# The second FFN product by sevens: results started by ScalarE, the residual added in the third to sixth products

## The chip, the core and the metric

The kernel is one program on one core of a Trainium2 chip. A core has five engines that run their own queues in order and meet through semaphores: TensorE (PE in the profile; its weight loads are shown as PEld), VectorE (DVE), ScalarE (ACT), GpSimd (POOL) and SyncE (SP, which here issues nearly all DMAs). The metric is the device time of one execution in microseconds (us); lower is better.

## What is computed

The reference is one layer of a hybrid decoder on 1024 prompt tokens and 64 sample tokens, all in float32, with D_MODEL = 1024 and D_FF = 2816:

```python
def swiglu(x, w_in, w_out):
    gu = x @ w_in
    g, u = gu[..., :D_FF], gu[..., D_FF:]
    return (jax.nn.silu(g) * u) @ w_out

x = x + 0.5 * swiglu(rmsnorm(x, norm_ffn1[l]), ffn1_w_in[l], ffn1_w_out[l])
mix, ... = token_mixing(rmsnorm(x, norm_mix[l]), ...)   # pooling branch and Mamba-2 SSD branch, gated
x = x + mix
x = x + 0.5 * swiglu(rmsnorm(x, norm_ffn2[l]), ffn2_w_in[l], ffn2_w_out[l])
y = rmsnorm(x, norm_final)
```

The change touches the last step of both FFNs: the product `(silu(g) * u) @ w_out`, its factor 0.5, and the residual `x + ...`.

## The kernel before

**Layout.** Activations stand transposed, features on the 128 partitions, tokens along the row. The 1088 tokens are held in two halves: h = 0 has 512 tokens, h = 1 has 576 (512 prompt tokens and the 64 sample tokens). A result of an FFN is therefore 8 row blocks m = 0..7 in two halves, 16 tiles `C[m, h]`.

**Precision.** Each float32 operand is split into a rounded high part and the remainder, and a product is three matmuls: high by high, low by high, high by low. The split of a tile costs one ACT instruction (the high part) and one DVE or POOL subtraction (the low part).

**Second product by sevens.** `second` (line 765) computes the product with 7 block products in place of 8 (a Strassen scheme over two halves of the features, of the outputs and of the tokens). The order is `ORDER2 = "4251736"`; in this document a product is called by its digit, so the first is "4" and the fifth is "7". Every product is done in two passes, m0 = 0 and m0 = 2. A pass runs over 11 contraction tiles kk in six steps of two (the last of one); per kk it has 12 matmuls of 272 columns, 132 in a pass, into four PSUM banks. Per FFN there are 14 passes, and the kernel has two FFNs.

What a pass needs and who brings it:

- Weights (`second_weights`, lines 745 to 763): for each step one or two 256 KB blocks are loaded by SP (line 751, tile `wraw`, 6 buffers); two blocks are added or subtracted on POOL (line 757, tile `ws`, 4 buffers; "3" and "4" need one block and no sum); ACT makes the high part `wh` (line 761) and DVE the low part `wl` (line 762), 3 buffers each.
- Operands (`fetch_x`, lines 770 to 791): for each kk one 272 KB tile is loaded by SP (line 784, tile `hr`, or `hp` for the products in `IN_PAIRS`, which have 8 tiles of their own for it), then split by ACT (line 774) and DVE, for "6" POOL (line 775). A product's 11 operands are loaded and split while the product before it runs. `hr` and its high part `hh` come from a pool of 42 tiles (`act`); one product without pairs takes 22 of them.
- Results (`add`, lines 800 to 807): after a pass, DVE adds each PSUM bank, times plus or minus 0.5, into one or two of the 16 tiles `C` (`scalar_tensor_tensor`, 10 or 12 instructions after a pass of most products, 120 for an FFN). `INTO2` says where a product goes. Since DVE only ever adds, `C` must hold the residual before the first result comes.
- Residual (`residual`, lines 793 to 798): it allocates the 16 tiles `C` (from the stage's pool `fx` of 17) and loads the saved x into them from `xspill` in DRAM, 8 loads of 256 KB and 8 of 288 KB, during "4"; both passes of "4" end with all their residual loads issued.

**Who sets the order.** The kernel keeps a small clock `pe[0]` of its own that counts 272/2400 us for a 272-column matmul (14.96 us for a pass) and interleaves generators by due times on it (`start`, `tick`): `X_AT` and `X_PACE` say when the next product's loads begin and how far apart they are, `X_LAG` how many loads a tile's split stays behind its own load. The tile framework then fixes each engine's queue when the program is built: an instruction goes into its queue when the framework expects its inputs and its buffers to be ready, and the earlier one in the code goes first where several are. On the chip each queue is then strictly in order: an instruction that waits holds all behind it.

**After the product.** When "7" is done, half 0 of the result is final and `after(0, ...)` is called; in FFN 1 that is `after1` (line 960), which starts the next RMSNorm of half 0 beside the last two products (`norm_parts`, line 937, with `rstd`, line 382: squares on ACT, their sums on DVE, a matmul with ones, a reciprocal root on POOL, and then for each of 8 tiles a scaling and a split). `HN_AT` and `HN_PACE` set its due times. When "3" is done, FFN 2 calls `half`.

Of the kernel before, what the change touches and what calls it, by code (L numbers as in the profile page):

```python
# [11 lines left out]
AF = mybir.ActivationFunctionType  # L12
ALU = mybir.AluOpType

P = 128
D = 1024
# [13 lines left out]
HALVES = (0, 1)  # L30
NTOK = (512, 576)
# [14 lines left out]
STEP_S = 1.0  # L46
POST, RIPE = 1.0, 3.0
GP = (1.5, 1.2)
HN_AT, HN_PACE = 3.0, 3.2
MP = 2.0  # L50
R_WAIT0 = 3.5
R_WAIT = 0.5
# [8 lines left out]
ORDER2 = "4251736"  # L61
# [3 lines left out]
INTO2 = {"1": ((0, 0, 1), (1, 1, 1)), "2": ((1, 0, 1), (1, 1, -1)), "3": ((0, 1, 1), (1, 1, 1)),  # L65
         "4": ((0, 0, 1), (1, 0, 1)), "5": ((0, 0, -1), (0, 1, 1)), "6": ((1, 1, 1),), "7": ((0, 0, 1),)}
IN_PAIRS = "457"
LO_POOL = "6"
X_AT, X_PACE, X_LAG = 4.0, 2.0, 2
SUM_PACE = 1.5  # L70


# [1 line left out]
def tile_hybrid_pool_ssd_macaron(  # L74
# [10 lines left out]
    V, S, T, G = nc.vector, nc.scalar, nc.tensor, nc.gpsimd  # L85
    dma = nc.sync.dma_start
# [7 lines left out]
    def nm(s):  # L94
        uid[0] += 1
        return f"{s}_{uid[0]}"

    def act(shape=(P, 576), dt=F32, name="a"):
        return sp.tile(list(shape), dt, tag="act", bufs=N_ACT, name=nm(name))

    def pair(n, name="hl"):
        t = sp.tile([P, 2, 576], F32R, tag="pair", bufs=N_PAIR, name=nm(name))
        return t[:, 0, :n], t[:, 1, :n], t
# [16 lines left out]
    def fx(dt=F32, name="x"):  # L120
        if stage["name"] == "mix":
            return act((P, 576), dt, name)
        return stage["p"].tile([P, 592], dt, tag="fx", bufs=N_FX, name=nm(name))
# [22 lines left out]
    def start(gen, delay=0.0):  # L146
        c = Chain(gen, delay)
        chains.append(c)
        return c
# [13 lines left out]
    def finish(c):  # L163
        while not c.done:
            c.step()
# [33 lines left out]
    def row_vec(src1d, n):  # L199
        rows.append((src1d, n))  # L200
        return sum(r[1] for r in rows[:-1])
# [3 lines left out]
    i_gm = row_vec(norm_mix[0], KD)  # L205
# [56 lines left out]
    xspill = [[dp.tile([P, NTOK[h]], F32, tag=f"xs{h}_{m}", name=f"xspill{h}_{m}") for m in range(KD)] for h in HALVES]  # L262
# [10 lines left out]
    xnd = [dp.tile([P, NTOK[0]], F32, tag=f"xn{k}", name=f"xnd{k}") for k in range(KD)]  # L273
# [490 lines left out]

    def second(wo, after, half):

        X, C = {p: [] for p in ORDER2}, {}
        n = 2 * NQ

        def fetch_x(p, kks, pace, lag=X_LAG):  # L770
            loaded = []

            def part_x(t, a):
                S.activation(a[:, :n], t[:, :n], AF.Identity)
                (G if p in LO_POOL else V).tensor_tensor(t[:, :n].bitcast(F32R), t[:, :n], a[:, :n].bitcast(F32), op=ALU.subtract)
                X[p].append((a, t.bitcast(F32R)))

            for kk in kks:
                if p in IN_PAIRS and kk < N_PAIR:
                    a, t, _ = pair(576, "hp")  # L780
                    t = t.bitcast(F32)
                else:
                    t, a = act((P, 576), F32, "hr"), act((P, 576), F32R, "hh")
                dma(t[:, :n], xq[p][kk])
                loaded.append((t, a))
                if len(loaded) > lag:
                    part_x(*loaded.pop(0))
                yield pace
            while loaded:
                part_x(*loaded.pop(0))  # L790
                yield pace

        def residual(ms):
            for m in ms:
                for h in HALVES:
                    C[m, h] = fx(name="x")
                    dma(C[m, h][:, : NTOK[h]], xspill[h][m])
                yield 1.0

        def add(pt, m, side, c, sign):  # L800
            if side:
                to = [(1, NA + NQ * c, 0, NQ)]
            else:
                to = [(0, 0, 0, NQ)] if c == 0 else [(0, NQ, 0, NQ - NA), (1, 0, NQ - NA, NA)]
            for h, at, of, w in to:
                o = C[m, h][:, at : at + w]
                V.scalar_tensor_tensor(o, pt[:, of : of + w], 0.5 * sign, o, op0=ALU.mult, op1=ALU.add)  # L807

        finish(start(fetch_x(ORDER2[0], range(NKK - 1), 0.0)))
        ahead = []  # L810
        for at, p in enumerate(ORDER2):
            if at + 1 < len(ORDER2):
                last = at + 2 == len(ORDER2)
                ahead.append(start(fetch_x(ORDER2[at + 1], range(NKK), 1.4 if last else X_PACE), 15.0 if last else X_AT if at else 6.0))
            for m0 in (0, 2):
                pts = [[psum("ps" if j and m0 and at < 5 else "pd", "po") for _ in range(2)] for j in range(2)]
                for kp in range(0, NKK, 2):
                    n2 = min(2, NKK - kp)
                    W2 = second_weights(wo, p, kp, n2, m0)
                    for j in range(2):  # L820
                        for k in range(n2):
                            while len(X[p]) <= kp + k:
                                ahead[at - 1].step()
                            xh, xl = X[p][kp + k]
                            for i, (w, x) in enumerate(((0, xh), (0, xl), (1, xh))):
                                for c in range(2):
                                    mm(pts[j][c][:, :NQ], W2[w][:, k, j * P : (j + 1) * P], x[:, c * NQ : (c + 1) * NQ],
                                       start=kp + k == 0 and i == 0, stop=kp + k == NKK - 1 and i == 2)
                            tick()
                    if at == 0 and kp == 2:  # L830
                        while summing:
                            finish(summing.pop())
                        if m0 == 0:
                            finish(start(fetch_x(p, range(NKK - 1, NKK), 0.0)))
                        res = start(residual((0, 4, 1, 5) if m0 == 0 else (2, 6, 3, 7)))
                if at == 0:
                    finish(res)
                with tc.high_priority(HP_EV):
                    for j in range(2):
                        for c in range(2):  # L840
                            for y, side, sign in INTO2[p]:
                                add(pts[j][c], 4 * y + m0 + j, side, c, sign)
            if p == "7":
                after(0, [C[m, 0] for m in range(KD)])
            if p == "3" and half:
                half(1, [C[m, 1] for m in range(KD)])
        after(1, [C[m, 1] for m in range(KD)])
# [86 lines left out]
            for k in range(4):  # L934
                dma(xspill[h][q * 4 + k], x[k][:, : NTOK[h]])

    def norm_parts(xt, h, gi, out, pace=1.0, away=None):

        N = NTOK[h]
        rr = []  # L940
        yield from rstd([t[:, :N] for t in xt], h, D, rr, pace)
        hi, lo, xn, hl = [], [], [], []
        for k in range(KD):
            x = fx(name="xn") if k >= 4 and not away else act((P, 576), name="xn")
            a, b, both = (act((P, 576), F32R, "hi"), act((P, 576), F32R, "lo"), None) if h else pair(576)
            V.scalar_tensor_tensor(x[:, :N], xt[k][:, :N], cols[:, gi + k : gi + k + 1], rr[0], op0=ALU.mult, op1=ALU.mult)
            split(x[:, :N], a[:, :N], b[:, :N])
            hi.append(a)
            lo.append(b)
            xn.append(x)  # L950
            hl.append(both)
            yield pace
            if away:
                dma(away[k], x[:, :N])
        out.append((h, hi, lo, xn, hl))

    wi1 = ffn1_w_in[0]
    prep1m = [None, None]

    def after1(h, xt):  # L960
        o = []
        if h == 0:
            prep1m[0] = start(norm_parts(xt, 0, i_gm, o, HN_PACE, xnd), HN_AT), o

        def away():
            for m in range(KD):
                dma(xspill[h][m], xt[m][:, : NTOK[h]])
                yield 2.0

        start(away(), 5.0)  # L970
        if h == 1:
            finish(prep1m[0][0])
            _, hi, lo, _, hl = prep1m[0][1][0]
            xn = [fx(name="xn") if k >= 4 else act((P, 576), name="xn") for k in range(KD)]
            for k in (0, 4, 1, 5, 2, 6, 3, 7):
                dma(xn[k][:, : NTOK[0]], xnd[k])
            prep1m[0][1][0] = (0, hi, lo, xn, hl)
            prep1m[1] = start(norm_parts(xt, 1, i_gm, o, 1.2), 0.5), o
# [814 lines left out]
    for h in HALVES:  # L1793
# [4 lines left out]
        if h == 1:  # L1798
            o = []
            prep2.append((start(norm_parts(reload(0), 0, i_g2, o, 2.0)), o))  # L1800
            c = prep2[0][0]
# [135 lines left out]
```

## Time and profile before

| | us |
|---|---|
| median of three runs | 2913.13 |
| the three runs | 2914.48, 2904.26, 2913.13 |
| the profiled execution, its own time | 2910.03 |
| span of its profile, first to last instruction | 2908.2 |
| PE busy in the span | 2790.9 (96%) |
| DVE / ACT / POOL busy | 1867.1 / 1396.1 / 1396.3 |

The span is what the profile's engines are measured in; the profiled execution took 1.8 us more than its span. The second product of FFN 1 runs from 528.20 to 794.32 us of the span, that of FFN 2 from 2627.48 to 2892.47. In the rows of the profile L12 means line 12 of the kernel printed above, `out<-in` names the tiles written and read, and an idle time is put down to the instruction or DMA that ended it.

### The profile page before, as it was taken

How to read it: one execution, taken by the hardware profiler on the slowest of the kernel's cores; microseconds unless marked ns; L12 is line 12 of the kernel's file. 1: busy time of each engine (PE TensorE's matmuls, PEld its weight loads, DVE VectorE, ACT ScalarE, POOL GpSimd, SP SyncE). 2: the span in 40 equal slices, each digit the busy share in tenths (PEclk: the TensorE clock that was granted, in tenths of full speed). 3: DMA queues.
4: the chain of work that ended last, by engine and by line, in shares of the span. 5: the costliest groups of instructions: out<-in, count | busy, mean ns of one | idle time of the engine just before them, and what ended most of it. 6: DMA issues, size and time to landing. Idle time of an engine off the chain costs nothing. (4 is left out here: it accounts for less than half of the span.)

```text
span 2908.2 us, 54642 instructions
## 1 busy us (share of the span) xinstructions
PE 2790.9 (96%) x19834; PEld 2613.8 (90%) x19834; DVE 1867.1 (64%) x2938; ACT 1396.1 (48%) x3070; POOL 1396.3 (48%) x1428
## 2 busy tenths in 40 slices
PE   7999999899999999999999999899999999998997
PEld 5999999898889999999988887678999999998997
DVE  6555555685784486876766776875665454557744
ACT  5444444443354555554556566566233434444433
POOL 6566667353642365554622332332135666673424
PEclk9999999999999999999999999899999999999999
DMA  4565554896745455554376677786765332338845
GB/s 138 178 206 195 171 167 142 275 290 209 226 122 167 141 174 169 173 160 135 102 239 215 197 233 234 253 259 185 249 234 166 102 105 90 97 120 299 281 147 173
DMA packets 515791, 539.49 MB, mean 186 GB/s; under 512 B 41780, under 2 KB 356008, under 8 KB 515512
## 3 DMA queue, kind: packets, MB, share of 16 engines
q1 hardware_dynamic: 515504, 535.99, 57.3%
q8 instruction: 156, 2.56, 0.4%
q14 instruction: 115, 0.94, 0.1%
q10 hardware_dynamic: 16, 0.00, 0.0%
HBM read 383.43 MB, written 152.65 MB: 184 GB/s over the span
## 5 line engine op out<-in xcount | busy, mean ns | idle before, releaser
L175 PE MATMUL pw<-X,wh 128*128 128x288 f32 (+2 forms) x2832 | 626.9, 310 | 4.3 <-ACT t L602 2.4
L175 PEld LDWEIGHTS pw<-X,wh 128*128 128x128 f32 x2832 | 462.2, 189 | 26.2 <-ACT t L602 2.9
L175 PE MATMUL pw<-X,wl 128*128 128x288 f32 (+1 forms) x1644 | 473.6, 288 | 0.7 <-DVE wl L457 0.7
L457 DVE TENSOR_TENSOR wl<-s,wh 128x512 fp32r<-128x512 f32 x288 | 242.5, 844 | 246.6 <-ACT wh L456 231.5
L175 PE MATMUL pw<-hl,wh 128*128 128x256 f32 (+1 forms) x1536 | 391.9, 328 | 3.4 <-ACT t L578 2.3
L450 POOL TENSOR_TENSOR s<-wraw,wraw 128x512 f32<-128x512 f32 x144 | 197.5, 1372 | 332.7 <-DVE wl L457 200.6
L175 PE MATMUL pw<-hi,wh 128*128 128x288 f32 x1120 | 331.8, 296 | 2.2 <-DVE t L614 1.5
L175 PE MATMUL pw<-hi,wl 128*128 128x288 f32 x1120 | 329.7, 294 | 0.0
L175 PE MATMUL pw<-lo,wh 128*128 128x288 f32 x1120 | 329.7, 294 | 0.0
L175 PEld LDWEIGHTS pw<-X,wl 128*128 128x128 f32 x1644 | 311.7, 190 | 0.9 <-DVE wl L457 0.9
L175 PE MATMUL pw<-hl,wl 128*128 128x256 f32 x1072 | 300.7, 281 | 1.0 <-DVE wl L457 1.0
L175 PEld LDWEIGHTS pw<-hl,wh 128*128 128x128 f32 x1536 | 259.0, 189 | 24.7 <-ACT t L578 2.9
L757 POOL TENSOR_TENSOR ws<-wraw,wraw 128x512 f32<-128x512 f32 x120 | 165.4, 1386 | 211.8 <-DMA wraw<-in_ffn_w_out_dram 115.4
L457 DVE TENSOR_TENSOR wl<-wraw,wh 128x512 fp32r<-128x512 f32 x216 | 180.1, 834 | 123.4 <-ACT wh L456 120.2
L456 ACT ACTIVATE wh<-s 128x512 fp32r<-128x512 f32 x288 | 181.0, 629 | 138.3 <-PE pw L175 112.2
L175 PEld LDWEIGHTS pw<-hi,wh 128*128 128x128 f32 x1120 | 210.5, 188 | 9.2 <-DVE t L614 2.1
L175 PEld LDWEIGHTS pw<-lo,wh 128*128 128x128 f32 x1120 | 210.6, 188 | 0.0
L175 PEld LDWEIGHTS pw<-hi,wl 128*128 128x128 f32 x1120 | 210.1, 188 | 0.0
L456 ACT ACTIVATE wh<-wraw 128x512 fp32r<-128x512 f32 x216 | 135.6, 628 | 153.7 <-PE pw L175 132.4
L175 PEld LDWEIGHTS pw<-hl,wl 128*128 128x128 f32 x1072 | 203.1, 189 | 2.0 <-DVE wl L457 2.0
L175 PE MATMUL po<-hh,wh 128*128 128x272 f32 x848 | 179.9, 293 | 6.5 <-ACT wh L761 4.5
L175 PE MATMUL pso<-yhl,wh 128*128 128x288 f32 (+1 forms) x768 | 177.8, 337 | 5.4 <-ACT acc L1727 4.5
(401 smaller groups left out, 6848.2 us busy)
## 6 DMA issues: line engine op xcount, KB each, us to landing
wraw<-in_ffn_w_out_dram SPq DMA_DIRECT2D x240, 256.0 KB
wraw<-in_ffn_w_in_dram SPq DMA_DIRECT2D x188, 256.0 KB
wraw<-in_w_in_dram SPq DMA_DIRECT2D x144, 256.0 KB
wh<-part SPq DMA_DIRECT2D x116, 256.0 KB
wl<-part SPq DMA_DIRECT2D x116, 256.0 KB
hr<-xq SPq DMA_DIRECT2D x106, 272.0 KB
xq<-s SPq DMA_DIRECT2D x66, 272.0 KB
xq<-g SPq DMA_DIRECT2D x62, 272.0 KB
```

The lines of the kernel that those rows point to most:

```text
L175: T.matmul(out, lhsT, rhs, start=start, stop=stop, skip_group_check=free)
L450: G.tensor_tensor(t, a, b, op=op)
L456: S.activation(wh, a, AF.Copy)
L457: V.tensor_tensor(wl, a, wh.bitcast(F32), op=ALU.subtract)
L757: G.tensor_tensor(s, raws[0], raws[1], op=ALU.subtract if p in MINUS2 else ALU.add)
```

## The change

Three things change in the second product, and one after it.

1. `C` is allocated at its first result. The first result of each (row block, half) is written by ScalarE, `S.activation(o, pt, AF.Copy, scale=0.5 * sign)`, and not added to anything; the later ones are added by DVE as before. Per FFN 40 of the 120 DVE instructions become ACT instructions: all 24 of "4", 8 of "2" and 8 of "5".
2. The residual is no longer loaded into `C` during "4". In the products "5", "1", "7" and "3" (third to sixth) it is loaded into a tile `xr` of the `act` pool, four tiles in each product, and added to `C` by a DVE `tensor_tensor` over the whole 512 or 576 columns: 16 loads and 16 DVE instructions per FFN. `RES2` says which four row blocks of which half. Due times: loads 3, 6, 12 and 18 us after the product's start on the kernel's clock, adds at 9, 15, 21 and 24.
3. `X_PACE` goes from 2.0 to 1.8 and `X_LAG` from 2 to 4: the next product's loads are closer together, and a tile is split four loads after its own and not two.
4. In FFN 1 the RMSNorm of half 0 gets shorter due times: 2.0 in place of 3.2 in `rstd` (`HN_R`), 3.0 in place of 3.2 in the eight scalings (`HN_PACE`).

```diff
-HN_AT, HN_PACE = 3.0, 3.2
+HN_AT, HN_PACE, HN_R = 3.0, 3.0, 2.0
...
+RES2 = {2: (0, (4, 5, 6, 7)), 3: (0, (0, 1, 2, 3)), 4: (1, (0, 1, 2, 3)), 5: (1, (4, 5, 6, 7))}
 LO_POOL = "6"
-X_AT, X_PACE, X_LAG = 4.0, 2.0, 2
+X_AT, X_PACE, X_LAG = 4.0, 1.8, 4
+RES_PACE = 3.0
...
-        def residual(ms):
-            for m in ms:
-                for h in HALVES:
-                    C[m, h] = fx(name="x")
-                    dma(C[m, h][:, : NTOK[h]], xspill[h][m])
-                yield 1.0
+        def residual(h, ms):
+            loaded = []
+            for m in ms + (None,):
+                if m is not None:
+                    t = act((P, NTOK[h]), name="xr")
+                    dma(t, xspill[h][m])
+                    loaded.append((m, t))
+                    yield RES_PACE
+                    if len(loaded) < 2:
+                        continue
+                m_, t = loaded.pop(0)
+                o = C[m_, h][:, : NTOK[h]]
+                V.tensor_tensor(o, o, t, op=ALU.add)
+                yield RES_PACE
...
+            new = (m, side) not in touched
+            if c:
+                touched.add((m, side))
             for h, at, of, w in to:
+                if (m, h) not in C:
+                    C[m, h] = fx(name="x")
                 o = C[m, h][:, at : at + w]
+                if new:
+                    S.activation(o, pt[:, of : of + w], AF.Copy, scale=0.5 * sign)
+                    continue
                 V.scalar_tensor_tensor(o, pt[:, of : of + w], 0.5 * sign, o, op0=ALU.mult, op1=ALU.add)
...
+            if at in RES2:
+                res = start(residual(*RES2[at]), 3.0)
             for m0 in (0, 2):
...
-                        res = start(residual((0, 4, 1, 5) if m0 == 0 else (2, 6, 3, 7)))
-                if at == 0:
-                    finish(res)
...
+            if at in RES2:
+                finish(res)
...
-        yield from rstd([t[:, :N] for t in xt], h, D, rr, pace)
+        yield from rstd([t[:, :N] for t in xt], h, D, rr, pace_r or pace)
...
-            prep1m[0] = start(norm_parts(xt, 0, i_gm, o, HN_PACE, xnd), HN_AT), o
+            prep1m[0] = start(norm_parts(xt, 0, i_gm, o, HN_PACE, xnd, HN_R), HN_AT), o
```

More of the change, by code (lines that the diff above doesn't have):

```diff
@@ L765, in second @@
     def second(wo, after, half):
-        X, C = {p: [] for p in ORDER2}, {}
+        X, C, touched = {p: [] for p in ORDER2}, {}, set()
         n = 2 * NQ
@@ L935, in turn_x, with norm_parts @@
                 dma(xspill[h][q * 4 + k], x[k][:, : NTOK[h]])
-    def norm_parts(xt, h, gi, out, pace=1.0, away=None):
+    def norm_parts(xt, h, gi, out, pace=1.0, away=None, pace_r=None):
         N = NTOK[h]
         rr = []
-        yield from rstd([t[:, :N] for t in xt], h, D, rr, pace)
+        yield from rstd([t[:, :N] for t in xt], h, D, rr, pace_r or pace)
         hi, lo, xn, hl = [], [], [], []
```

## The prediction

> **What bounds the kernel now.** I began with the page: the span and the busy shares.
>
> ```profile
> span 2908.2 us, 54642 instructions
> PE 2790.9 (96%) x19834; PEld 2613.8 (90%) x19834; DVE 1867.1 (64%) x2938; ACT 1396.1 (48%) x3070; POOL 1396.3 (48%) x1428
> ```
>
> PE sets the time: it is busy for 96% of the span, and no other engine has more than 64%. No matmul is added or removed, so the change can gain only where PE waits inside the two second products, or runs there at a lower clock. To find these places I asked for busy time by stretches, for the instructions on the result tile `po` alone, with one stretch for each pass (from its first matmul to the first of the next). The columns are the stretch, its length, busy time and instructions of PE, PEld and DVE, the granted clock, the DMA share and GB/s. FFN 1 first, then the two longest of FFN 2 and its sum.
>
> ```profile
> 544.91:569.82 24.91, 18.88 (x135) 18.01 (x133) 3.28 (x12) 0.93 1.05 360
> 569.82:587.56 17.74, 17.17 (x135) 16.88 (x134) 3.27 (x13) 1.00 0.99 321
> 587.56:604.28 16.72, 16.72 (x135) 16.72 (x134) 2.84 (x10) 1.00 0.87 277
> ...
> 655.48:673.03 17.55, 17.42 (x135) 16.85 (x133) 3.00 (x10) 1.00 0.89 288
> 673.03:699.48 26.45, 19.80 (x134) 19.26 (x133) 3.24 (x11) 0.81 0.63 195
> ...
> 750.93:771.15 20.22, 17.40 (x135) 16.96 (x133) 2.18 (x7) 0.99 0.76 247
> 771.15:794.32 23.17, 20.25 (x133) 19.49 (x132) 1.56 (x5) 0.79 0.76 234
> sum 266.12, PE 245.37 PEld 241.29 DVE 35.16; mean PE 17.53 PEld 17.24 DVE 2.51
> ...
> 2645.18:2669.78 24.60, 19.07 (x135) 18.35 (x133) 3.36 (x12) 0.93 1.05 365
> 2773.05:2798.62 25.57, 19.33 (x134) 18.90 (x133) 3.24 (x11) 0.87 0.57 180
> sum 264.99, PE 245.27 PEld 239.42 DVE 35.56; mean PE 17.52 PEld 17.10 DVE 2.54
> ```
>
> An undisturbed pass takes 16.72 us (the third row). All 28 passes take 266.12 + 264.99 = 531.11 us against 28 x 16.72 = 468.16, so 62.95 us is all that could be won. Three places hold most of it: the second pass of "4" (8.19 and 7.88 over 16.72), the first of "7" (9.73 and 8.85), and both passes of FFN 1's "6" (3.50 and 6.45).
>
> **The wait in "4".** What PE waited for in that pass; SP's queue ahead of it; and the DMAs of the same 25 us.
>
> ```profile
> PE po L175 <- ACT wh L761: 6.0, 3, 3.0
> ...
> 547.63 0.38 SPq L751 DMA_DIRECT2D wraw<-in_ffn_w_out_dram  x1
> 548.30 1.72 SPq L784 DMA_DIRECT2D hr<-xq  x3
> 550.42 2.59 SPq L797 DMA_DIRECT2D x<-xspill  x4
> 553.44 0.32 SPq L784 DMA_DIRECT2D hr<-xq  x1
> 554.19 0.38 SPq L751 DMA_DIRECT2D wraw<-in_ffn_w_out_dram  x1
> ...
> DMA packets 4917, 8.76 MB, mean 350 GB/s; under 512 B 494, under 2 KB 1261, under 8 KB 4916
> q1 hardware_dynamic: 4916, 8.74, 100.8%
> hr<-xq SPq DMA_DIRECT2D x12, 272.0 KB
> x<-xspill SPq DMA_DIRECT2D x8, 288.0 KB
> x<-xspill SPq DMA_DIRECT2D x8, 256.0 KB
> ```
>
> PE waits for the high part of a weight tile. Its load was late: SP issues two weight loads 6.56 us apart with eight others between, while the 16 DMA engines are full (100.8% at 350 GB/s). Half of those bytes are the residual: 8 x 288 KB + 8 x 256 KB = 4.46 MB of 8.76, or 12.7 us at 350 GB/s.
>
> **The wait in "7".** ACT's queue (in brackets its idle time and what ended it) and what PE waited for, in the first pass of "7".
>
> ```profile
> 669.12 0.61 ACT L761 ACTIVATE wh<-ws 128x512 fp32r<-128x512 f32 x1
> 672.35 0.66 ACT L774 ACTIVATE hh<-hr 128x544 fp32r<-128x544 f32 x1 [2.62 <-DMA hr<-xq]
> 674.44 0.66 ACT L774 ACTIVATE hh<-hr 128x544 fp32r<-128x544 f32 x1 [1.43 <-DMA hr<-xq]
> 679.17 0.66 ACT L774 ACTIVATE hh<-hr 128x544 fp32r<-128x544 f32 x1 [4.08 <-DMA hr<-xq]
> 679.74 1.65 ACT L761 ACTIVATE wh<-ws 128x512 fp32r<-128x512 f32 x3
> ...
> PE po L175 <- ACT wh L761: 4.2, 1, 4.2
> PE po L175 <- DVE wl L762: 2.5, 1, 2.5
> ```
>
> Here bytes are not short (share 0.63). ACT stands before three operand splits of "3" whose loads come late, and three weight splits of "7" queue behind them. PE idles 4.2 + 2.5 = 6.7 us; the other 3.0 of the 9.73 is the lower clock after it (0.81).
>
> **The change, part by part.** All is reckoned against the profiled execution, 2910.03 us (span 2908.2 and 1.8 around it); the median of the three runs is 3.1 above it, and I do not add that, since it lies within their spread.
>
> *Residual loads leave "4".* The 16 loads go from ahead of the late weights into four later products; with them 12.7 us of DMA time goes from a stretch of 25 us. The operand loads (12 of 272 KB, 9.5 us by the same rate) fit beside the weight loads. That `C` is allocated at its first result costs nothing: it takes the same 16 of 17 tiles, later than now. In return ACT, and no longer DVE, empties the banks of "4", 12 instructions after each pass. Prices of the two kinds of instruction, first the present add, then an ACT copy from PSUM of 288 columns, then a DVE add of two SBUF tiles as the new residual add is, last the waits of the present add for its residual:
>
> ```profile
> L807 DVE SCALAR_TENSOR_TENSOR x<-po,x x240: 173/424/442, 544.6 to 2892.9; 128x272 f32<-128x272 f32 x72, 128x240 f32<-128x240 f32 x32, 128x32 f32<-128x32 f32 x16
> L612 ACT COPY t<-pw x40: 379/382/404, 109.7 to 2623.7; 128x288 f32<-128x288 f32 x40
> L393 DVE TENSOR_TENSOR ssq<-ssq,sq x52: 673/744/1812, 701.4 to 2152.0; 128x512 f32<-128x512 f32 x26, 128x576 f32<-128x576 f32 x26
>   DMA x<-xspill: 4.6, 6
> ```
>
> Twelve at most at 0.38 us hold ACT for 4.6 us. PE uses a weight tile for 16.72 / 5.5 = 3.04 us and has two more ahead, 6.1 us of cover, so this is hidden as the DVE burst is today; the passes after a burst lose 1.02 ("2", first) and 0.83 ("1", second). I leave 1.0 in each: 8.19 + 7.88 - 2.0 = **14.1 us gained**. Ends: 16.1 if nothing is left, 0 if the operand loads take the freed DMA time.
>
> *Loads four ahead.* The last operand load moves from 4 + 10 x 2.0 = 24 to 22 on the kernel's clock, 2 x 16.72/14.96 = 2.2 us. Against it, four residual loads of 288 KB (1.18 MB, 3.4 us at 350 GB/s) enter the stretch before "7", where SP runs about a pass ahead. That stretch is 17.55 us at share 0.89, so 1.9 us of it is free: 1.5 us is not. Net 0.7 us earlier. The `xr` tiles also take up to four of the 42 `act` tiles, of which "1" (22) and "7" (6) leave 14 for "3"; the longer lag lets the loads take free tiles ahead of the splits, so I let these cancel. ACT's order (operand splits ahead of weight splits) I take as unchanged, so the wait stays, shorter by that and some of its cold clock: 1.1 us each, **2.2 us gained**. Ends: 18.6 gained if the order tips over, 6.8 lost if 3.4 us comes on top twice.
>
> *Residual adds.* The 80 DVE adds that go to ACT are at most 0.42 each, 34 us in all; 32 adds of 0.74 come, 24 us, or 58 at 1.81. DVE's total hardly moves at the medians. But each new add waits in DVE's queue with `wl` behind it: 4.6/6 = 0.77 us by the nearest row, 4.08 at worst (the longest operand wait before "7"), so 1.5 to 5.9 us against 6.1 of cover. If the cover is used up, an add is worth half of a ten-add burst (3.0 us of DVE, up to 1.02 of PE), 0 to 0.5 us. I take 0.1 each, 3.2 us, less 1.2 for shorter bursts after "2" and "5" (6 adds in place of 10): **2 us lost**; ends 1 gained, 16 lost.
>
> The Trainium skill (SBUF — State Buffer, section "Who interferes with whom") speaks against this part: a DVE instruction with two SBUF inputs and a GpSimd instruction that reads SBUF exclude each other, while one with a single SBUF input is free. The trace agrees: the PSUM add stays under 0.45 us, the two-input add goes from 0.67 to 1.81. If every second new add met a weight sum on POOL, 16 x 1.07 = 17 us of DVE would come, an estimate, and at a third of that for PE the sum would end 6 us higher.
>
> *Norm due times (FFN 1 only).* Rows of all engines (PE, PEld, DVE, ACT, POOL busy, clock, DMA share, GB/s) around the end of FFN 1:
>
> ```profile
> 733.00:750.00 17.00, 17.00 (x138) 17.00 (x137) 8.09 (x15) 4.71 (x9) 7.98 (x8) 1.00 0.69 217
> 750.00:774.00 24.00, 20.00 (x147) 19.24 (x146) 23.78 (x29) 9.64 (x17) 17.66 (x12) 0.93 0.72 233
> ```
>
> DVE is full in "6" (23.78 of 24) and half idle before. `rstd` has six waits that shrink by 1.2, 7.2 on the kernel's clock or 8.0 us. A third (8 of 24) of the norm's work leaves the full stretch: a third of the 9.95 lost there, **3 us gained**; ends 8 gained, 2 lost.
>
> Sum: 2910.03 - 14.1 - 2.2 + 2 - 3 = 2892.7, **2893 us**.
>
> **The rivals.** *The wait of "7" goes too.* For it: the three late splits come from a close race between loads and weight splits, and it looks alike in both FFNs, so it is one order that either stands or tips. Against: the new loads enter right there. Gain 18.6 - 2.0 = 16.6 in place of 2.2: **2878 us**.
>
> *The load is moved, not removed.* The middle products are nearly full already:
>
> ```profile
> DMA packets 16781, 20.01 MB, mean 290 GB/s; under 512 B 1274, under 2 KB 13267, under 8 KB 16773
> q1 hardware_dynamic: 16773, 19.91, 89.2%
> ```
>
> These are the 69 us from 604 to 673. Free is 10.8%, 7.5 us; the residual of "5" and "1" and, by SP's lead, some of "7" is 2.1 to 3.3 MB, at 290/0.892 = 325 GB/s 6.5 to 10 us. If it does not fit, weights come late once per FFN as in "4" today, or the framework issues the loads as early as now: 2893 + 14.1 = **2907 us**.
>
> *Slower: the adds stop DVE.* An add whose load is late holds `wl` beyond the cover, as operands do to ACT before "7". It decides from 17.3/32 = 0.54 us of PE per add. Two such stalls per FFN, one in "5" or "1" and one in "7" or "3", at the 9.3 us of "7" today: 2893 + 37 = **2930 us**. For it: DMAs at 0.80 to 1.00 share around "5" and "1". Against: loads stand 6 or 9 us ahead of their adds on the kernel's clock.
>
> **How the numbers follow.** Forecast (2884 to 2901) 0.45; "7" goes too (2868 to 2884) 0.20; moved, not removed (2901 to 2918) 0.23; slower (2918 to 2940) 0.12. The range 2868 to 2918 leaves out the last, and some 0.05 below and above the others. A measurement of this kernel can tell about 0.5% from no change: below 2898.6 is faster and above 2927.7 slower, from the median of 2913.13. Faster: 0.20 and 0.38 of the forecast's 0.45, 0.58. Slower: 0.08 of the 0.12. Same: the rest, 0.34.
>
> **What would show it.** Right: the second pass of "4" under 18.5 us in both FFNs with a DMA share below 0.9; no residual load before "2"; the first pass of "7" still between 23 and 27; DVE waits for `xr` loads of under 1 us each; FFN 1's "6" shorter by some 3 us in all. Wrong: a pass of "5", "1" or "3" above 19 us; SP issuing `xr` loads between the weights of "4"; ACT's first writes ahead of `wh` with PE waiting; any other stage of the kernel longer by more than a few us, since all queues are laid out anew.

## The result and the profile after

| | before | after |
|---|---|---|
| median of 19 runs each, us | 2910.97 | 2899.47 |
| lowest to highest, us | 2904.26 to 2914.91 | 2892.66 to 2906.40 |
| profiled execution, us (span) | 2910.03 (2908.2) | 2906.40 (2904.6) |

The ratio is 0.996, with a 95% interval of 0.9952 to 0.9968: 11.5 us less. The interval leaves out 1, but the gain is under the 0.5% that the prediction called faster; by that bound the answer is "same". The profiled execution of the changed kernel was the slowest of its 19. So I profiled the same program once more (span 2895.9, called the second profile below), and I trust a difference between stages only where both show it.

First the page of the changed kernel, its span and its busy shares.

```profile
span 2904.6 us, 54721 instructions
PE 2788.6 (96%) x19834; PEld 2607.3 (90%) x19834; DVE 1878.8 (65%) x2890; ACT 1413.8 (49%) x3150; POOL 1400.8 (48%) x1428
```

PE still sets the time with the same 19834 matmuls; ACT has 80 instructions more, DVE 48 fewer (80 left, 32 came). Now the passes that the prediction spoke of, by stretches for the instructions on `po`. The columns are as before, with ACT's busy time added behind DVE's, since ACT now writes results too: length, PE, PEld, DVE, ACT, clock, DMA share, GB/s. FFN 1: second pass of "4", second of "5", first of "1", first of "7", both of "6". FFN 2: second of "4", second of "5", first of "1", first of "7", second of "3".

```profile
545.43:565.20 19.77, 18.10 (x134) 16.83 (x133) 0.00 (x0) 2.63 (x12) 1.00 0.95 314
616.38:636.48 20.10, 18.25 (x132) 16.93 (x132) 1.60 (x6) 1.55 (x4) 1.00 0.89 282
636.48:655.41 18.93, 17.80 (x132) 16.97 (x133) 1.60 (x6) 1.24 (x4) 1.00 0.82 259
672.13:692.37 20.24, 17.70 (x134) 16.87 (x133) 2.75 (x10) 0.00 (x0) 1.00 0.71 230
744.43:770.49 26.06, 19.86 (x135) 18.83 (x133) 2.86 (x8) 0.00 (x0) 0.87 0.69 210
770.49:787.54 17.05, 17.05 (x134) 16.73 (x132) 1.47 (x4) 0.00 (x0) 1.00 0.98 317
2641.72:2661.66 19.94, 17.87 (x135) 16.84 (x133) 0.00 (x0) 2.63 (x12) 1.00 0.91 296
2714.07:2733.77 19.70, 18.15 (x135) 16.85 (x133) 1.60 (x6) 1.54 (x4) 1.00 0.87 287
2733.77:2752.22 18.45, 17.45 (x133) 16.93 (x134) 1.60 (x6) 1.24 (x4) 1.00 0.78 253
2768.94:2794.64 25.70, 20.04 (x135) 19.50 (x134) 3.25 (x11) 0.00 (x0) 0.80 0.63 204
2831.44:2850.89 19.45, 17.23 (x135) 16.73 (x133) 5.71 (x16) 0.00 (x0) 1.00 0.90 306
```

Against the rows of before:

| pass | FFN 1 before, after | FFN 2 before, after |
|---|---|---|
| "4", second | 24.91, 19.77 | 24.60, 19.94 |
| "5", second | 17.76, 20.10 | 17.47, 19.70 |
| "1", first | 16.72, 18.93 | 16.72, 18.45 |
| "7", first | 26.45, 20.24 | 25.57, 25.70 |
| "6", first | 20.22, 26.06 | 23.05, 21.22 |
| "6", second | 23.17, 17.05 | 16.71, 16.72 |

"4" gains 5.1 and 4.7 us, 9.8 in all. "5" and "1" give 8.5 of that back: 2.3 and 2.2 in FFN 1, 2.2 and 1.7 in FFN 2. "7" is 6.2 us shorter in FFN 1 and not at all in FFN 2. In "6" of FFN 1 the loss changes passes. The whole products, of the first profile and then of the second, one row for each FFN:

```profile
528.73:787.54 258.81, 243.69 (x1848) 237.05 (x1848) 22.82 (x76) 10.97 (x40) 0.99 0.81 261
2624.06:2888.83 264.77, 246.13 (x1848) 238.17 (x1848) 23.52 (x78) 10.96 (x40) 0.98 0.70 230
```
```profile
529.44:786.10 256.66, 242.83 (x1848) 236.37 (x1848) 22.81 (x76) 10.94 (x40) 0.99 0.80 263
2618.55:2880.16 261.61, 245.97 (x1848) 238.44 (x1848) 23.52 (x78) 10.95 (x40) 0.98 0.70 233
```

Before they took 266.12 and 264.99, so the two products gained 7.5 us in the first profile and 12.8 in the second, most of it in FFN 1: 7.3 and 9.5 there, 0.2 and 3.4 in FFN 2. The work between them took 1833.2 us before and 1836.5 and 1832.5 in the two profiles of after: the same program differs there by 4 us from one execution to the next, and I read nothing into that.

### The profile page after: what moved, and what is told of

Read it like the earlier page. It is cut to its first block, busy times and chain, and to the rows that moved or that the text cites. A ratio compares the mean times of both kernels' runs of the same rounds, so it can differ in the third digit from the quotient of the medians.

```text
span 2904.6 us, 54721 instructions
## 1 busy us (share of the span) xinstructions
PE 2788.6 (96%) x19834; PEld 2607.3 (90%) x19834; DVE 1878.8 (65%) x2890; ACT 1413.8 (49%) x3150; POOL 1400.8 (48%) x1428
## 5 line engine op out<-in xcount | busy, mean ns | idle before, releaser
L177 PE MATMUL po<-hh,wl 128*128 128x272 f32 x848 | 178.9, 292 | 8.3 <-DVE wl L764 7.7
```

Of the source, the lines that this page charges most:

```text
L177: T.matmul(out, lhsT, rhs, start=start, stop=stop, skip_group_check=free)
```

## The experiments

Eleven other kernels were run, and the changed one once more, in three groups of four on one chip each, always against the kernel before. Ratios are of time to before, with 95% intervals.

| run | what it is | ratio | interval |
|---|---|---|---|
| e_res | before + residual part alone | 0.9965 | 0.9951 to 0.9978 |
| e_ahead | before + loads closer and four ahead | 0.9954 | 0.9942 to 0.9966 |
| e_lag | before + four ahead, pace as before | 0.9956 | 0.9943 to 0.9968 |
| e_norm | before + norm due times alone | 0.9994 | 0.9984 to 1.0004 |
| e_nonorm | after, norm due times as before | 0.9965 | 0.9955 to 0.9975 |
| e_nores | after, residual left out | 0.9910 | 0.9897 to 0.9922 |
| e_adds | after, adds kept, 16 loads made one | 0.9921 | 0.9906 to 0.9937 |
| e_loads | after, loads kept, adds on 8 columns | 0.9954 | 0.9940 to 0.9967 |
| e_no7 | after, no residual loads in "7" | 0.9968 | 0.9956 to 0.9979 |
| e_light | e_nonorm, residual spread by free DMA time | 0.9922 | 0.9908 to 0.9935 |
| e_light6 | e_light, six ahead | 0.9934 | 0.9920 to 0.9948 |
| a_again | after, once more | 0.9962 | 0.9948 to 0.9975 |

**Each part alone.** `e_res` takes the diff without its constants for `X_PACE`, `X_LAG` and the norm; `e_ahead` and `e_norm` are the opposite (`e_norm` also has the two lines of the change that pass `HN_R` on):

```diff
-X_AT, X_PACE, X_LAG = 4.0, 2.0, 2      # e_ahead
+X_AT, X_PACE, X_LAG = 4.0, 1.8, 4
-HN_AT, HN_PACE = 3.0, 3.2              # e_norm
+HN_AT, HN_PACE, HN_R = 3.0, 3.0, 2.0
```

> The residual part alone (first results written by ACT, residual loaded and added in the third to sixth products), with operand loads two ahead at pace 2.0 and the norm's due times as before. Kernel before about 2911 us, changed kernel 2899.5. Theory A, the gain is the residual leaving the first product: about 2900 to 2903, the second pass of '4' near 19.8 us in both FFNs, '7' first pass near 25 us in both. Theory B, the residual's loads only move their stall into '5' and '1' (their second and first pass now about 2 us longer each), and the gain comes from loads four ahead: about 2907 to 2911 here.

> The kernel before with operand loads four steps ahead at pace 1.8, nothing else changed. Theory A (the residual part carries the gain): 2908 to 2913, the first pass of '7' still 25 to 26 us in both FFNs, the second pass of '4' still near 24.8. Theory B (four ahead carries it): 2898 to 2904, with the first pass of '7' near 20 us in one FFN or both.

> The kernel before with the shorter due times of the first half's norm alone. Prediction's term: 3 us gained in FFN 1's '6', 2908. Theory from the new profile: the second pass of '6' gets 6 us shorter and the first 6 us longer, so no change: 2910 to 2912.

Two constants, with the residual left as it was, gain 0.46% (2906.37 to 2893.47 us, 12.9). The passes of `e_ahead` (columns as in the prediction): second of "4" in FFN 1, first of "7" in FFN 1 and in FFN 2.

```profile
543.40:568.20 24.80, 19.70 (x134) 19.27 (x133) 3.20 (x12) 0.86 1.06 368
672.73:689.88 17.15, 17.08 (x132) 16.86 (x133) 3.24 (x11) 1.00 0.74 242
2763.77:2782.41 18.64, 18.57 (x133) 18.34 (x133) 3.25 (x11) 0.91 0.64 208
```

"4" is as long as before. "7" is 9.3 and 6.9 us shorter; that is where the gain is. ACT's queue in `e_ahead` at FFN 1's "7" (start, length, idle time before it in brackets):

```profile
671.50 0.66 ACT L774 ACTIVATE hh<-hr 128x544 fp32r<-128x544 f32 x1 [3.79 <-DMA hr<-xq]
672.07 0.61 ACT L761 ACTIVATE wh<-ws 128x512 fp32r<-128x512 f32 x1
672.59 0.64 ACT L774 ACTIVATE hh<-hr 128x544 fp32r<-128x544 f32 x1
673.13 1.14 ACT L761 ACTIVATE wh<-ws 128x512 fp32r<-128x512 f32 x2
```

Before, ACT stood three times for operands (2.62, 1.43 and 4.08 us) and the weight splits of "7" came behind the third. Here there is one long wait (3.79), it ends before "7" begins at 672.73, and weight splits stand between the operand splits: the order of ACT's queue is another one.

The residual part alone shortens "4" as the change does (18.91 and 18.14) and, which I had not foreseen, "7" too, with the operands still two ahead (first pass, FFN 1 and 2):

```profile
671.21:690.83 19.62, 18.28 (x135) 16.99 (x134) 3.00 (x10) 0.00 (x0) 1.00 0.83 271
2762.04:2782.23 20.19, 17.67 (x134) 16.84 (x133) 2.99 (x10) 0.00 (x0) 1.00 0.71 240
```

How it does that can be seen in ACT's queue at FFN 1's "7", which begins at 671.21:

```profile
673.67 0.61 ACT L763 ACTIVATE wh<-ws 128x512 fp32r<-128x512 f32 x1
...
680.12 0.66 ACT L776 ACTIVATE hh<-hr 128x544 fp32r<-128x544 f32 x1 [3.46 <-DMA hr<-xq]
680.68 0.61 ACT L763 ACTIVATE wh<-ws 128x512 fp32r<-128x512 f32 x1
```

The operand loads are no earlier than before (SP issues the last two from 676.95, against 673.70 for the last one before), and ACT still stands 3.46 us for a late one. But weight splits now stand between the operand splits (at 673.67, 674.74 and 680.68), where before none did from 669.73 to 679.74. The passes of theory B came too: the second of "5" takes 19.84 and 18.76 us and the first of "1" 17.86 and 19.03, 6.8 us more than before in all. The time still went with theory A.

The norm's due times do nothing to the time (0.9994). Alone they do to "6" of FFN 1 what they did in the changed kernel; the row of its two passes in `e_norm`:

```profile
749.43:773.57 24.14, 19.04 (x133) 18.29 (x133) 2.87 (x8) 0.86 0.69 228
773.57:790.26 16.69, 16.69 (x134) 16.63 (x132) 1.48 (x4) 1.00 0.92 295
```

The loss of 3.50 and 6.45 becomes 7.4 and nothing: 40.83 us in place of 43.39. In the time that cannot be told from nothing, the interval reaching from 4.7 us gained to 1.2 lost. `e_nonorm`, the changed kernel with the old due times, agrees: 0.9965 against 0.996.

> The changed kernel with the norm's old due times (residual part and loads four ahead together). The parts alone stand at 0.9965 and 0.9954. If the norm's due times spoil the combination: 0.991 to 0.9935, with FFN 1's '6' at 20 and 23 us. If the two parts themselves do not add, since the residual's loads refill the stretch that four-ahead had cleared: 0.995 to 0.997, first pass of '7' again 20 to 26 us.

**Pace or lag.** `e_lag` changes only `X_LAG` (2 to 4) in the kernel before.

> The kernel before with the split four loads behind (X_LAG 4) and the old pace 2.0; with both it stood at 0.9954. If the lag does it: 0.9945 to 0.9965 and '7' first pass under 19 us. If the shorter pace does it: 0.998 to 1.001 and '7' first pass near 25 us.

It gains what `e_ahead` does, 0.9956, so the lag carries it and the closer loads carry nothing that can be measured. Its "7" is 7.8 us shorter than before in FFN 1 and 7.4 in FFN 2; the row of FFN 1:

```profile
672.87:691.51 18.64, 18.56 (x133) 18.35 (x133) 3.25 (x11) 0.91 0.67 219
```

ACT's queue has the order that it has in `e_ahead`, with one wait of 4.13 us that ends at 671.64. And the loads themselves go out earlier, at the old pace. SP's issues of the last operand loads of "3" in FFN 1, before and then in `e_lag`:

```profile
673.70 0.41 SPq L784 DMA_DIRECT2D hr<-xq  x1
...
668.02 0.84 SPq L784 DMA_DIRECT2D hr<-xq  x2
```

Before, the last one is issued 0.67 us after "7" has begun (673.03); with the lag both are out 4 us before it begins (672.87). Why a longer lag brings the loads forward was not tried.

**Why the parts do not add.** 0.9965 and 0.9954 would give 0.992; together they give 0.9965 (`e_nonorm`), or 0.996 with the norm. First, both gain in "7". By the rows of `e_res` and `e_ahead` the lag had only 19.62 - 17.15 = 2.5 and 20.19 - 18.64 = 1.5 us left to win there, 0.14%, which makes 0.995. Second, in FFN 2 not even that came: 25.70 us where `e_res` took 20.19. (`e_nonorm`, both parts with the old norm, has 19.50 and 24.38.) The missing 0.0015 lies within the intervals, so it is this row, and not the time, that shows the second reason. In the changed kernel's FFN 2, ACT's queue and then SP's (which issues the loads) at the first pass of "7":

```profile
2764.37 0.63 ACT L763 ACTIVATE wh<-ws 128x512 fp32r<-128x512 f32 x1 [2.08 <-POOL ws L759]
2764.91 1.79 ACT L776 ACTIVATE hh<-hr 128x544 fp32r<-128x544 f32 x3
2774.99 0.66 ACT L776 ACTIVATE hh<-hr 128x544 fp32r<-128x544 f32 x1 [8.29 <-DMA hr<-xq]
2775.55 0.61 ACT L763 ACTIVATE wh<-ws 128x512 fp32r<-128x512 f32 x1
```
```profile
2757.40 0.34 SPq L800 DMA_DIRECT2D xr<-xspill  x1
2758.18 1.83 SPq L786 DMA_DIRECT2D hr<-xq  x3
2760.43 4.66 SPq L753 DMA_DIRECT2D wraw<-in_ffn_w_out_dram  x6
2765.30 0.33 SPq L800 DMA_DIRECT2D xr<-xspill  x1
2769.49 0.89 SPq L753 DMA_DIRECT2D wraw<-in_ffn_w_out_dram  x2
2770.47 1.37 SPq L786 DMA_DIRECT2D hr<-xq  x3
```

A single operand split holds ACT for 8.29 us, twice the longest wait that the prediction's rows show. It ends at 2774.99, so by its time the load is one of the three that SP issues from 2770.47, behind two residual loads, eight weight loads and a gap from 2765.6 to 2769.5. In that gap SP stands for a buffer: its longest wait there, 2.7 us before a weight load, is put down to the weight sum on POOL, and this sum began at 2767.67 after waiting 3.43 us for its own weights, while the DMA engines were full (share 1.01 from 2755 to 2769). The wait that the lag had removed is back, with residual loads among what stands ahead of the late load. The test is to leave the residual out (`RES2 = {}`) or to move its loads away from "7":

```diff
-RES2 = {2: (0, (4, 5, 6, 7)), 3: (0, (0, 1, 2, 3)), 4: (1, (0, 1, 2, 3)), 5: (1, (4, 5, 6, 7))}
+RES2 = {}                                                        # e_nores
+RES2 = {2: (0, (4, 5, 6, 7), 3.0), 3: (0, (0, 1, 2, 3), 3.0),    # e_no7
+        5: (1, (0, 1, 2, 3, 4, 5, 6, 7), 1.5)}    # third entry: the residual's pace
```

> The changed kernel with the residual left out of both FFNs (no loads of xspill in the second product, no adds of it; the output lacks the residual). The difference to the changed kernel is what residual loads and adds cost in their new place. Theory A: they are nearly hidden, 0 to 4 us, so 2895 to 2899. Theory B: they cost the 4 us per FFN that '5' and '1' became longer, and more in '4' to '7': 2885 to 2891, with '5' second pass and '1' first pass back to 16.7 to 17.8 us.

> The changed kernel with one group moved: the four residual tiles loaded in '7' go to '3', which then has all eight of half 1 at half the pace; those of '5' and '1' stay. The changed kernel stands at 0.996 of the kernel before. Theory: these four loads alone make the operands of '3' late before '7', so the first pass of '7' falls below 18 us in both FFNs and the time to 0.992 to 0.9945. Rival: the loads of '5' and '1' push everything behind them, so '7' stays at 20 to 26 us and the time at 0.995 to 0.997.

"7" in `e_nores`, FFN 1 and 2, is undisturbed:

```profile
667.91:684.63 16.72, 16.72 (x135) 16.72 (x133) 3.13 (x11) 0.00 (x0) 1.00 0.64 207
2752.75:2769.47 16.72, 16.72 (x134) 16.72 (x133) 2.99 (x11) 0.00 (x0) 1.00 0.59 193
```

Its second pass of "5" takes 17.46 and 18.32 us and its first of "1" 18.33 and 17.12, so not all are back under 17.8 as theory B had it: of the 8.5 us lost in "5" and "1", some 6 go away with the residual and some 2.5 do not.

`e_no7` nearly clears "7" too, 18.82 and 18.18 us where the theory asked for less than 18; but the time, 0.9968, came out where the rival had put it. Two passes of its FFN 2, the first of "7" and the second of "3":

```profile
2768.38:2786.56 18.18, 16.97 (x134) 16.76 (x133) 3.24 (x11) 0.00 (x0) 1.00 0.70 225
2823.40:2844.49 21.09, 17.29 (x135) 16.76 (x133) 5.75 (x16) 0.00 (x0) 0.99 0.93 317
```

In FFN 2 "7" is 7.5 us shorter than in the changed kernel and the whole product 5.7 (259.09 against 264.77; 2.5 against the second profile); 1.6 went back in "3". In FFN 1 "7" gains 1.4, while the second passes of "2" (18.57) and "1" (18.56) lose 1.5 and 1.8 against 17.08 and 16.72 there. These are one execution's; the work between the products was 4.5 us longer in it than in the second profile, which by what is said above may be chance. So why the time did not follow in full is only partly settled.

**Loads or adds.** `e_nores` shows that the residual in its new place costs 0.5% (0.996 against 0.991). `e_adds` keeps the 16 adds but loads one tile per FFN for all of them; `e_loads` keeps the loads and cuts each add to 8 columns (in both, as in `e_nores`, the residual or most of it is left out of the result).

```diff
+        one = act((P, 576), name="xr")                            # e_adds
+        dma(one, xspill[1][0])
-                    dma(t, xspill[h][m])
-                    loaded.append((m, t))
+                    loaded.append((m, one[:, : NTOK[h]]))
-                V.tensor_tensor(o, o, t, op=ALU.add)              # e_loads
+                V.tensor_tensor(o[:, :8], o[:, :8], t[:, :8], op=ALU.add)
```

> The changed kernel with the 16 residual adds per FFN, but one tile loaded once per FFN in place of 16 loads (the output lacks the right residual). Relative to the kernel before, the changed kernel stands at 0.996 and the one without residual at 0.991. Theory L, the loads cost it (bytes in products whose DMA is full): 0.991 to 0.9925. Theory D, the adds in DVE's queue cost it: 0.995 to 0.997.

> The changed kernel with all its residual loads, but each add done on 8 of the 512 or 576 columns only (the output lacks most of the residual), so that DVE still waits for each load but works about 0.1 us and not 0.7. Theory L (loads cost): 0.995 to 0.997, first pass of '7' in FFN 2 still about 25 us. Theory D (DVE's time costs): 0.991 to 0.9925.

Against `e_nores` the loads cost 0.44%, 12.8 us, and the adds 0.11%, 3.2 us. Each carries some 5 to 6 us of uncertainty (the root of the two half-widths' squares), so the loads do cost and the adds cannot be told from nothing. The whole product of FFN 1 takes 254.31 us in `e_adds` and 254.94 in `e_loads`, that of FFN 2 252.74 and 260.23. The first pass of "7" in FFN 2, of `e_adds` and then of `e_loads`, and ACT's long wait in the latter:

```profile
2754.59:2772.13 17.54, 16.97 (x134) 16.75 (x133) 3.24 (x11) 0.00 (x0) 1.00 0.60 200
2757.86:2782.80 24.94, 19.10 (x135) 18.62 (x133) 3.25 (x11) 0.00 (x0) 0.86 0.64 212
...
2763.23 0.66 ACT L776 ACTIVATE hh<-hr 128x544 fp32r<-128x544 f32 x1 [7.54 <-DMA hr<-xq]
```

With the loads the wait before one operand split is there (7.54 us, 8.29 in the changed kernel); with the adds and no loads it is not. So it is the residual's loads (with the tiles that they hold), and not its adds, that bring the wait back.

**A better place for the loads.** `e_light` spreads the loads by where DMA time is free: half 0 two tiles per product from "2" to "7", and all eight of half 1 in "3", which needs one weight block per step where its neighbours need two; the norm as before. `e_light6` adds two to its lag.

```diff
+RES2 = {1: (0, (4, 5), 6.0), 2: (0, (6, 7), 6.0), 3: (0, (0, 1), 6.0), 4: (0, (2, 3), 6.0),
+        5: (1, (0, 1, 2, 3, 4, 5, 6, 7), 1.5)}
-X_AT, X_PACE, X_LAG = 4.0, 1.8, 4                                # e_light6
+X_AT, X_PACE, X_LAG = 4.0, 1.8, 6
```

> As the run before (old norm due times, four ahead), with the residual of half 0 two tiles at a time in '2', '5', '1' and '7' and all eight tiles of half 1 in '3', whose weights are half as many bytes. Theory L (bytes in full products cost): 0.991 to 0.9935, '5' second pass and '1' first pass back under 18 us and '7' first pass under 20. Theory D or no effect of place: 0.995 to 0.997; worse if '3' now overflows, its passes over 18 us.

> The version with the residual in the light products (0.9922 of the kernel before), with the split six loads behind. If late operands still hold ACT in it (96 us of waits for hr and hp in its profile): 0.988 to 0.991. If four was enough: 0.991 to 0.9935. Worse than 0.994 if splits come too late for the next product.

`e_light` takes 0.9922 of before (0.9908 to 0.9935), 2885.59 us: it beats both kernels, and its interval lies clear of `e_nonorm`'s, from which it differs in `RES2` and the pace given there alone. In its rows (first of "7" in FFN 1, first of "7" and second of "3" in FFN 2) "7" is nearly free in both FFNs, and "3" pays for it:

```profile
667.58:685.45 17.87, 16.96 (x134) 16.74 (x133) 3.24 (x11) 0.00 (x0) 1.00 0.68 222
2758.30:2775.02 16.72, 16.72 (x134) 16.72 (x133) 3.24 (x11) 0.00 (x0) 1.00 0.83 255
2811.86:2832.97 21.11, 17.28 (x135) 16.78 (x133) 5.74 (x16) 0.00 (x0) 1.00 0.95 315
```

"7" is most of the gain: the two products together are 11.5 us shorter than `e_nonorm`'s (510.17 against 521.70), and 9.3 of that lies in the first passes of "7". The rest of what theory L foretold came in one of four passes: the second of "5" takes 19.06 and 20.07 us and the first of "1" 17.16 and 18.64, where under 18 was expected. Nor is the room in "3" enough: `e_no7` has the same eight tiles there, and its time is 0.9968. `e_light` differs from it by two tiles in each of four products in place of four in each of two, and by the norm's due times. Which of these helps, and why, no run separates.

Six ahead (0.9934) is no better than four: "7" is free (16.97 and 16.72), but the first pass of "6" takes 27.86 us in FFN 1 and 24.26 in FFN 2.

> The changed kernel once more, for a second profile beside the first, which was of its slowest execution (2906.4 us of 2892.66 to 2906.4). Near 0.996; in its profile the first pass of '7' 20 to 26 us, '5' second and '1' first pass 18 to 20.

The repeat, 0.9962, agrees with the 0.996 of the 19 runs; its two rows stand above.

## Why the prediction was right or wrong

I forecast 2893 us, range 2868 to 2918; measured is 2899.47, in the range and at the edge of the forecast's own part (2884 to 2901). The sum came near because its errors have both signs: that the time was met is in part luck, and one of its four terms rests on a step that was wrong.

- *Residual loads leave "4"*: right in kind, 14.1 us expected, 9.8 measured (10.5 in the second profile's 19.98 and 19.05). PE's wait in FFN 1's pass for the high part of a weight tile fell from 6.0 us to 0.7. But the pass is not under 18.5 and its DMA share not under 0.9. What is left there is not the residual: in FFN 1's pass 13 weight and 10 operand loads keep the share at 0.95 (314 GB/s), and `e_nores` still takes 19.08 us in FFN 2.
- *The load is moved, not removed* (0.23): its price, all 14.1 given back, was too high, its mechanism true in part. "5" and "1" pass 19 us or come near it in both FFNs, 8.5 us lost where the sum had no more than part of the 2 us for its adds. By `e_nores` some 6 of it are the residual's.
- *Loads four ahead*: wrong. The step "ACT's order ... I take as unchanged, so the wait stays" failed, and with it the term of 2.2 us. In the kernel before, the lag and the pace are worth 12.9 us (`e_ahead`) and the lag alone 13.6 (`e_lag`). Two things were wrong in the step. The order does tip: the trace shows weight splits between the operand splits, and the long operand wait over before "7" begins. And I reckoned the last load 0.7 us earlier, from the pace; in `e_lag`, at the old pace, it is issued 5 us earlier. `e_res`, where "7" is 6.8 us shorter with operand loads that are no earlier, speaks for the order by itself; no run changes it alone.
- *The wait of "7" goes too* (0.20): true of the lag in the kernel before, true by two thirds in FFN 1 here, false in FFN 2. I had named the reason against it ("the new loads enter right there"), but had taken both FFNs as one order that stands or tips. They went different ways.
- *Residual adds*: 2 us expected; the residual costs some 14.5 (0.996 against 0.991). I looked for the cost in the adds. That is the wrong place: `e_adds` costs a quarter of what `e_loads` does. DVE's waits for residual loads, in the changed kernel, and who waited for the adds themselves:

```profile
L807 DVE TENSOR_TENSOR x<-x,xr x32: 676/746/1849, 590.3 to 2841.4; 128x512 f32<-128x512 f32 x16, 128x576 f32<-128x576 f32 x16
...
  DMA xr<-xspill: 23.0, 10
who waited for it (us, times):
  ACT wh L763: 2.4, 1
```

  Ten adds waited 2.3 us each, against "under 1" foretold, and ACT waited 2.4 us once on an add. In `e_loads` DVE waits as much (22.2 in 9) and its adds are short. Whether the loads cost by their bytes, by the `act` tiles that they hold, or by DVE waiting for them, the runs do not separate; `e_adds` takes away all three at once.
- The Trainium skill (SBUF — State Buffer, "Who interferes with whom") let me reckon 6 us more for two-input adds that meet GpSimd. The trace agrees that some do: 6 of the 32 adds take 1.41 to 1.85 us, and each of these begins while a weight sum runs on POOL; the other 26 take 0.68 to 0.76, ten of them overlapped by a sum that begins later. So it was 6, not the 16 of my estimate, some 6 us of DVE and not 17. `e_adds` puts all that the adds cost at 3.2 us, with an uncertainty that covers both nothing and the 6.
- *Norm due times*: 3 us expected, 0.9994 measured, from which neither 3 us nor nothing can be told. By the rows of single executions the term is there: FFN 1's "6" takes 40.83 us in `e_norm` against 43.39, and 43.11 in the changed kernel against 46.15 in `e_nonorm`. What the sum left out is that four ahead makes "6" longer (46.10 in `e_ahead`, 2.7 more than before). In the changed kernel the loss moves from the second pass of "6" to the first and the two together lose 43.11 - 33.44 = 9.7 us, 9.95 before.
- *Slower: the adds stop DVE* (0.12): did not happen. No pass of "5", "1" or "3" lost 9 us.
- Of the other signs, four came out as on the side of "right": no residual load is issued before "2" (the first of FFN 1 at 585.82 us, in its second pass) or between the weights of "4"; the pass behind ACT's first writes, the first of "2", loses 0.4 us over 16.72 where it lost 1.0; and the rest of the program is as long as before, within the 4 us told above.
- By places, then: 9.8 for 14.1 in "4"; 6.1 (first profile) for 2.2 in "7"; 8.5 lost in "5" and "1" and 2.2 in "3" of FFN 2, for 2 lost; 0.3 for 3 in FFN 1's "6".
- The chance of 0.58 for faster by 0.5% took most of the forecast's own part to lie below 2898.6. Measured is 2899.47, 0.9 us above that bound, and the gain of 0.4% lies in "same" (0.34).

## What to carry to other kernels

Where an in-order engine makes tiles for two streams, put the instructions whose inputs come late behind the ones that are ready: two more steps between a load and its use were worth as much here as the whole change (and brought the last loads forward, too). A part that gains alone can spoil another through a queue that they share, so time the parts alone and together. When loads leave a crowded stretch, look at what stands behind them in the queue where they go: here four tiles at a time in "5", "1", "7" and "3" made one late operand split hold ACT for 8.29 us, and two at a time, with the rest in "3", were worth 11 us more.

## What the runs showed that I had not expected

- Moving the residual out of "4" shortened "7", four products later, by 6.8 and 5.4 us with operand loads still two ahead. The trace shows weight splits between the late operand splits of ACT's queue; no run changes that order alone.
- The two FFNs run the same code on the same shapes; after the change the same pass took 20.24 us in one and 25.70 in the other, and in the second profile 19.30 and 25.45:

```profile
672.50:691.80 19.30, 17.68 (x134) 16.86 (x133) 2.99 (x10) 0.00 (x0) 1.00 0.72 239
2762.34:2787.79 25.45, 20.38 (x135) 19.84 (x133) 3.25 (x11) 0.00 (x0) 0.80 0.64 209
```

  It repeats, so it belongs to the order laid out when the program is built, not to the execution.
